# Up-projection weight factors on Trainium2: the low part made by ScalarE and an accumulating DMA in place of a VectorE subtraction

## The chip, the cores and the metric

The kernel runs on one core of one Trainium2 chip. A core has a matrix engine (TensorE, "PE" in the profile; "PEld" is its weight load), a vector engine (VectorE, "DVE"), an engine for functions of one input (ScalarE, "ACT"), GpSimd ("POOL") and SyncE ("SP"), which here only issues transfers. Transfers run on 16 DMA engines; they are issued from an engine's queue in that queue's order, and a queue whose next transfer has to wait holds back all those behind it. The metric is the time of one execution on the device in microseconds (us). Of the kernel before there are three runs: 2419.17, 2419.81 and 2420.04 us; the median is 2419.81 us.

## What is computed

A decoder layer over 2048 positions of width 1024, in float32: a first half (projections, a pooling mixer, windowed attention, gates, an output projection) and a feed-forward half. The change touches the feed-forward half's up-projection:

```python
h = rmsnorm(x, ffn_norm)                                 # (2048, 1024)
up = causal_depthwise_conv(h @ w_up, conv_w, conv_b)     # w_up: (1024, 5632), window 3
gate, val = up[..., :2816], up[..., 2816:]
x = x + (silu(gate) * val) @ w_down
```

## The kernel before

**Two parts of each number.** TensorE is fed with a reduced format (`fp32r`). A float32 number goes in as a high part (the number rounded to that format) and a low part (the number minus its high part), and a product takes three matmuls: high with high, high with low, low with high. High parts come from ScalarE as a copy that rounds (CAST); low parts come from VectorE as a subtraction of the high part from the number.

**Stages.** The 2048 positions are done in two chunks of 1024 (`c` = 0 and 1). Each chunk runs the first half of the layer, the output projection (`out_proj`), the up-projection (`up`) and the down-projection (`Down`). In the profiled execution the up-projection of chunk 0 lies at about 590 to 990 us and that of chunk 1 at about 1785 to 2195 us; the output projection of chunk 0 lies ahead of it, from about 500 us.

**One unit of the up-projection.** `up` goes over 22 units `f`. A unit takes one 128-column slab of `w_up` for the gate (`g`, 128 x 1024 numbers, 512 KB) and one for the value (`v`, likewise), and multiplies them with the normed input by a scheme of seven block products in place of eight (`one` to `seven`, 12 matmuls of 128 x 512 each). The weight side of the scheme needs factors in two parts: `A11, A12` from `g`; `A22` from the half of `v`; `S3, S2` from `v` after two in-place subtractions; and `S1, S4` from `g` after two in-place operations. Class `Blocks` makes them in four steps: `first` (A11, A12), `second` (A22, then L354 and L355 change `v` in place), `third` (S3, S2), `fourth` (L362 and L363 change `g` in place, then S1, S4). The steps `first`, `third` and `fourth` call `halved`, which takes a tile `U` of 128 x 2 x 1024, writes the high part into its first half on ScalarE (L334) and the low part into its second half on VectorE (L335). `second` splits half a slab with lines of its own (L350, L351).

**Order of the work.** In the loop over the units the four steps for unit `f+1` are called between the products of unit `f` (`weights(f + 1, 1)`), so each factor is made about a unit before the products that read it. The program is written in that order, and a scheduler places each instruction in its engine's queue; each engine then works through its queue in order, waiting on semaphores.

**Buffers and queues.** Raw slabs land in pool `rp` (tag `R`, 3 buffers); a buffer is loaded anew when its last reader has finished. All transfers of this part are issued from SP's queue by `load` (L215): the slabs (`R<-w_up`), the stored activations (`actd<-M`), and in the output projection the residual input (`F<-xT`), the weights (`R<-w_out`) and `x2d<-M`. GpSimd issues none.

**The two first units of chunk 0.** Units 0 and 1 (`PRE`) are treated apart. In chunk 0 their slabs are loaded during the output projection into one `U` tile each (`U<-w_up`), `Blocks` makes their factors there (two steps per output tile), and `store` writes the factors to device memory from SP's queue (`kept<-U`, `kept<-M`), from where both chunks fetch them (`U<-kept`). So `halved` runs 6 times in the output projection of chunk 0 and 3 times for each of 20 units in each chunk: 126 times.

Of the kernel before, what the change touches and what calls it, by code (L numbers as in the profile page):

```python
# [16 lines left out]
F32 = mybir.dt.float32  # L17
F32R = mybir.dt.float32r
I32 = mybir.dt.int32
U8 = mybir.dt.uint8  # L20
AF = mybir.ActivationFunctionType
ALU = mybir.AluOpType
# [172 lines left out]
def block_kernel(ctx: ExitStack, tc: tile.TileContext, x, xT, pos, vec, qkn, w_poolT, w_pool, w_q, w_kv,  # L195
                 w_gp, w_ga, w_out, w_up, w_down, outT):
    nc = tc.nc
    V, G, A = nc.vector, nc.gpsimd, nc.scalar
# [18 lines left out]
    def split(hi, lo, src):  # L217
# [4 lines left out]
            low = V.tensor_sub(lo[:, t], src[:, t], hi[:, t].bitcast(F32))  # L222
        return high.ins, low.ins

    def halves(h, t, src, gain):

        A.activation(h[:, 0, t], src, AF.Identity, scale=gain)
        V.scalar_tensor_tensor(h[:, 1, t], src, gain, h[:, 0, t].bitcast(F32), op0=ALU.mult,
                               op1=ALU.subtract)
# [84 lines left out]
    class Blocks:  # L314
# [16 lines left out]
        def halved(self, first, second, raw):  # L331
            t = up_.tile([P, 2, 8, P], F32R, "U")
            self.tiles.append(t)
            A.copy(t[:, 0], raw)  # L334
            V.tensor_sub(t[:, 1], raw, t[:, 0].bitcast(F32))  # L335
            self.w[first], self.w[second] = t[:, :, 0:4], t[:, :, 4:8]

        def step(self, n=1):
# [52 lines left out]
    raw = [rp.tile([P, 8, P], F32, "R") for _ in range(3)] + [mp.tile([P, 8, P], F32, "M")]  # L391
# [18 lines left out]
    def make_h(c, n, hs, ks=range(KT)):  # L410

        a, b = ((0, 256), (256, 512), (512, T))[n] if c == 0 else (0, T)
        t, w = slice(a, b), b - a
        for k in ks:
            if n == 0:
                hs.append(up_.tile([P, 2, T], F32R, "U"))
            if c == 0:
                src = xs0[k // 2][:, k % 2, t]
            else:
                src = mp.tile([P, w], F32, "M")  # L420
                load(src, xT[k * P:(k + 1) * P, c * T:(c + 1) * T])
            halves(hs[k], t, src, vc[:, V_AN + k:V_AN + k + 1])
# [1184 lines left out]
```

## Time and profile before

| What | before |
|---|---|
| median of 3 runs | 2419.81 us (2419.17 to 2420.04) |
| span of the profiled execution | 2416.4 us, first to last instruction; what lies around it to the median is 3.4 us |
| TensorE busy | 2397.1 us, 99% |
| VectorE busy | 1885.1 us, 78% |
| ScalarE busy | 1121.3 us, 46% |
| GpSimd busy | 156.2 us, 6% |
| granted TensorE clock | 0.999 of full |
| high part of `halved`, ScalarE L334 | 126 of 128 x 1024, about 1.05 us each |
| low part of `halved`, VectorE L335 | 126 of 128 x 1024, about 1.22 us each |

Reading the rows: a row of a list of windows gives the stretch and its length, then for each engine the time that it was busy and the number of its instructions, then the granted TensorE clock, the mean busy share of the 16 DMA engines and the rate that they moved. A row of the timeline gives start and duration in us, the engine, the line, the operation, output and input, and in brackets the idle time just before with what ended it. "SPq" is SP's queue issuing. TensorE's matmuls are pipelined, so the ends of its rows overlap the next starts.

### The profile page before, as it was taken

To read this page: it belongs to the slowest core of one execution; us is meant where nothing else is said; L and a number is where in the kernel's file an instruction comes from. 1 tells how busy PE (TensorE), PEld (TensorE's weight loads), DVE (VectorE), ACT (ScalarE), POOL (GpSimd) and SP (SyncE) were. 2 spreads that over 40 slices of the span, in tenths; PEclk is the share of its full clock that TensorE was granted. 3 is DMA by queue.
4 is the path that set the end of the run, shared out by engine and by line. 5 is a ranking of instruction groups with operands and counts; after the bars stand their busy time and mean duration, and the time that the engine had idled before them with its cause. 6 is when DMAs were issued, how large, how long until landed. Compare 5 with 4: busy or idle time off the path is not lost.

```text
span 2416.4 us, 30417 instructions
## 1 busy us (share of the span) xinstructions
PE 2397.1 (99%) x11252; PEld 1994.5 (83%) x11252; DVE 1885.1 (78%) x3011; ACT 1121.3 (46%) x2150; POOL 156.2 (6%) x102
## 2 busy tenths in 40 slices
PE   8999999999999999999999999999999999999999
PEld 8878888888888888788888888888888888888887
DVE  8687788765988788899956867665479878889994
ACT  7445444444554555543523433333445445554432
POOL 1113111000000000000002221110000000000000
PEclk9999999999999999999999999999999999999999
DMA  9755354268222233644334542131642222228421
GB/s 343 245 188 169 137 183 156 101 227 283 79 87 88 96 105 109 220 155 153 119 143 126 169 167 98 65 108 54 208 164 95 87 87 79 79 70 287 139 70 52
DMA packets 139028, 337.84 MB, mean 140 GB/s; under 512 B 12289, under 2 KB 48641, under 8 KB 127873
## 3 DMA queue, kind: packets, MB, share of 16 engines
q1 hardware_dynamic: 138448, 335.72, 40.8%
q8 instruction: 88, 1.44, 0.2%
q14 instruction: 60, 0.48, 0.1%
q10 hardware_dynamic: 432, 0.19, 0.0%
HBM read 231.67 MB, written 104.20 MB: 139 GB/s over the span
## 4 chain that ended last, share of the span: by engine, by line
PE 93%; DVE 3%; ACT 2%; DMA 1%; issue 1%; POOL 0%; SPq 0%; DVEq 0%; ACTq 0%; POOLq 0%
PE f L238 34%; PE f L1105 19%; PE t L1105 10%; PE a L1105 5%; PE f L1406 4%; PE a L1406 4%; PE s L1406 4%; PE t L1406 4%; PE a L887 2%; PE s L826 2%; PE a L238 1%; PE t L859 1%; DMA U<-actd 0%; DMA U<-w_down 0%; DVE F L941 0%
## 5 line engine op out<-in xcount | busy, mean ns | idle before, releaser
L238 PE MATMUL f<-U,U 128*128 128x512 f32 (+1 forms) x3936 | 916.7, 390 | 3.5 <-DVE U L222 1.9
L238 PEld LDWEIGHTS f<-U,U 128*128 128x128 f32 x3936 | 727.4, 188 | 153.6 <-DVE U L222 4.3
L1105 PE MATMUL f<-U,U 128*128 128x512 f32 x1512 | 359.8, 390 | 1.3 <-ACT Q L1123 1.3
L1105 PEld LDWEIGHTS f<-U,U 128*128 128x128 f32 x1512 | 283.4, 188 | 61.6 <-ACT Q L1123 2.2
L1171 DVE SCALAR_TENSOR_TENSOR M<-F,vc,M 128x1024 f32<-128x1024 f32 x176 | 225.2, 1282 | 126.1 <-ACT M L1168 125.7
L1105 PE MATMUL t<-U,U 128*128 128x512 f32 x1080 | 253.8, 389 | 0.9 <-ACT Q L1123 0.9
L1105 PEld LDWEIGHTS t<-U,U 128*128 128x128 f32 x1080 | 202.6, 188 | 43.4 <-ACT Q L1123 1.4
L845 ACT ACTIVATE Q<-s,st,rq 128x128 f32<-128x128 f32 x256 | 113.8, 455 | 105.9 <-DVE st L842 104.0
L334 ACT CAST U<-R 128x1024 fp32r<-128x1024 f32 x120 | 125.4, 1053 | 60.3 <-DVE R L363 29.7
L335 DVE TENSOR_TENSOR U<-R,U 128x1024 fp32r<-128x1024 f32 x120 | 146.4, 1222 | 0.0
L1105 PE MATMUL a<-U,U 128*128 128x512 f32 x576 | 139.0, 390 | 0.0
L1105 PEld LDWEIGHTS a<-U,U 128*128 128x128 f32 x576 | 108.0, 188 | 22.4
L867 POOL TENSOR_SCALAR_AFFINE_SELECT M<-M 128x1024 fp32r<-128x1024 f32 x64 | 90.6, 1416 | 542.1 <-DVE M L864 343.5
L1105 PE MATMUL f<-U,M 128*128 128x512 f32 x504 | 122.0, 390 | 0.5 <-DVE F L1149 0.5
L1364 ACT CAST U<-U 128x1024 fp32r<-128x1024 f32 x76 | 79.1, 1050 | 80.6 <-PE a L1406 25.6
L1105 PEld LDWEIGHTS f<-U,M 128*128 128x128 f32 x504 | 94.5, 188 | 20.9 <-DVE F L1149 1.3
L1168 ACT ACTIVATE M<-F,vc 128x1024 f32<-128x1024 f32 x88 | 109.4, 1243 | 1.9 <-DVE F L1153 0.5
L1157 ACT COPY F<-f 128x512 f32<-128x512 f32 x42 | 24.6, 587 | 171.0 <-PE f L1105 171.0
L222 DVE TENSOR_TENSOR U<-R,U 128x512 fp32r<-128x512 f32 x142 | 95.0, 700 | 6.9 <-ACT U L221 6.2
L1365 DVE TENSOR_TENSOR U<-U,U 128x1024 fp32r<-128x1024 f32 x76 | 92.0, 1219 | 6.3 <-ACT U L1364 6.1
L221 ACT CAST U<-R 128x512 fp32r<-128x512 f32 x142 | 80.7, 618 | 20.4 <-PE f L238 8.2
L1364 ACT CAST F<-U 128x1024 fp32r<-128x1024 f32 x44 | 46.2, 1050 | 91.4 <-PE a L1406 58.6
(273 smaller groups left out, 3620.8 us busy)
## 6 DMA issues: line engine op xcount, KB each, us to landing
R<-w_up SPq DMA_DIRECT2D x80, 512.0 KB, 3.7
actd<-M SPq DMA_DIRECT2D x44, 512.0 KB, 2.6
U<-w_down SPq DMA_DIRECT2D x88, 256.0 KB, 5.0
U<-actd SPq DMA_DIRECT2D x88, 256.0 KB, 5.4
qd<-U SPq DMA_DIRECT2D x64, 256.0 KB, 3.7
Q<-qd SPq DMA_DIRECT2D x64, 256.0 KB, 4.1
R<-w_out SPq DMA_DIRECT2D x32, 512.0 KB, 5.3
U<-kept SPq DMA_DIRECT2D x12, 1024.0 KB, 7.1
```

Of the source, the lines that this page charges most:

```text
L222: low = V.tensor_sub(lo[:, t], src[:, t], hi[:, t].bitcast(F32))
L238: nc.tensor.matmul(out, a, b, start=(i == 0), stop=(i == n - 1))
L334: A.copy(t[:, 0], raw)
L335: V.tensor_sub(t[:, 1], raw, t[:, 0].bitcast(F32))
L845: A.activation(pr[:, h, :], sc[:, h, 0:P], AF.Exp, bias=nm[:, h:h + 1], scale=it["rq"][:, h:h + 1], accum_out=rs[:, h:h + 1])
L867: G.affine_select(own.rearrange("p a h q -> p (a h) q"), pa.bitcast(F32).rearrange("p a h q -> p (a h) q"), pattern=[[0, 8], [1, P]], base ...
L1105: nc.tensor.matmul(bank, a[:, x, k, :], b[k // 2][:, y, k % 2, :], start=(first and i == 0), stop=(i == 11), skip_group_check=True)
L1168: A.activation(y, u[:, 2:], AF.Identity, bias=cw[:, 3, m:m + 1], scale=cw[:, 2, m:m + 1])
L1171: V.scalar_tensor_tensor(y, u[:, j:j + T], cw[:, j, m:m + 1], y, op0=ALU.mult, op1=ALU.add)
L1364: A.copy(hi, src)
L1365: V.tensor_sub(lo, src, hi.bitcast(F32))
L1406: nc.tensor.matmul(into[m], u[:, 0, c_], v[:, 1], start=(first and j == 0), stop=(k == n - 1 and j == 2), skip_group_check=True)
```

## The change

`halved` calls a new function `parts_added` in place of the ScalarE copy and the VectorE subtraction. ScalarE still writes the high part; then ScalarE reads the raw numbers a second time, multiplies by -1 and writes the rounded result, which is the negated high part, into the place of the low part; then GpSimd issues a DMA with `accum_op=ALU.add` that adds the raw numbers (viewed as `fp32r`) onto it. The sum is the raw number minus its high part. `second` keeps its VectorE subtraction.

```diff
+    def parts_added(hi, lo, src):
+
+        A.copy(hi, src)
+        A.activation(lo, src, AF.Copy, scale=-1.0)
+        G.dma_start(lo, src.bitcast(F32R), accum_op=ALU.add)
+
...
         def halved(self, first, second, raw):
             t = up_.tile([P, 2, 8, P], F32R, "U")
             self.tiles.append(t)
-            A.copy(t[:, 0], raw)
-            V.tensor_sub(t[:, 1], raw, t[:, 0].bitcast(F32))
+            parts_added(t[:, 0], t[:, 1], raw)
             self.w[first], self.w[second] = t[:, :, 0:4], t[:, :, 4:8]
```

In the changed file the new lines are L227 (high part), L228 (negated high part) and L229 (the DMA); lines behind them stand 6 further down, those behind `halved` 5.

**ScalarE, one unit of the steady up-projection.** Before, in ScalarE's queue (L334 are the three high parts, `third`, `fourth` and the next unit's `first`; L350 is A22's; L1123 empties PSUM banks; L1161 and L1166 carry two columns; L1168 and L1182 belong to the convolution and the gate):

```order
L350 CAST M_6967<-R_6672 128x512
L1123 COPY Q_6984<-f_6913 128x512
L1161 COPY F_7047<-uh_193 128x2
L334 CAST U_6986<-R_6672 128x1024
L1166 COPY uh_193<-F_6775 128x2
L1168 ACTIVATE M_7003<-F_6775,vc_127 128x1024
L1123 COPY Q_7030<-t_7017 128x512
L334 CAST U_7014<-R_6670 128x1024
L334 CAST U_7082<-R_6806 128x1024
L1182 ACTIVATE M_7007<-M_7003 128x1024
```

The same stretch of a unit in the changed kernel (L355, L1128, L1166, L1171, L1173 and L1187 are the lines above, shifted by 5):

```order
L355 CAST M_7276<-R_6974 128x512
L1128 COPY Q_7293<-f_7221 128x512
L1166 COPY F_7358<-uh_193 128x2
L227 CAST U_7295<-R_6974 128x1024
L228 ACTIVATE U_7295<-R_6974 128x1024
L1171 COPY uh_193<-F_7080 128x2
L1173 ACTIVATE M_7313<-F_7080,vc_127 128x1024
L227 CAST U_7324<-R_6972 128x1024
L228 ACTIVATE U_7324<-R_6972 128x1024
L1128 COPY Q_7341<-t_7328 128x512
L227 CAST U_7393<-R_7111 128x1024
L1187 ACTIVATE M_7317<-M_7313 128x1024
```

Each cast has gained a second pass behind it (that of the third cast stands behind the gate's L1187); the rest keeps its order.

**GpSimd, the steady up-projection.** Its queue was empty there; now it holds three accumulating DMAs per unit, each waiting for ScalarE and for an earlier DMA of its own kind:

```order
L229 DMA U_6420<-R_6138 128x1024 [waits DMASW5_49,DMAHW0_49,PE_49,Activation_49]
L229 DMA U_6461<-R_6140 128x1024 [waits DMASW7_49,DVE_49,DMAHW2_49,PE_49,Activation_49]
L229 DMA U_6490<-R_6138 128x1024 [waits DVE_49,DMASW6_49,PE_49,Activation_49]
L229 DMA U_6559<-R_6277 128x1024 [waits DMASW0_49,DMAHW3_49,PE_49,Activation_49]
L229 DMA U_6600<-R_6279 128x1024 [waits DMASW2_49,DVE_49,DMAHW5_49,PE_49,Activation_49]
```

"DMASW" are the semaphores of DMAs that GpSimd issued, "DMAHW" those of SP's.

**SP, the output projection of chunk 0.** The stores of unit 1's factors and what stands behind them, before:

```order
L215 DMA kept_0_47_5275<-U_5177 128x2048 [waits DMAHW2_49,Activation_49]
L215 DMA x2d_208<-M_5259 128x512 [waits DMAHW3_49,DVE_49]
L215 DMA kept_1_48_5277<-M_5180 128x1024 [waits DMAHW4_49,Activation_49]
L215 DMA kept_2_49_5279<-U_5226 128x2048 [waits DMAHW5_49,Activation_49]
L215 DMA kept_3_50_5281<-U_5231 128x2048 [waits DMAHW6_49,Activation_49]
L215 DMA x2d_208<-M_5308 128x512 [waits DMAHW7_49,DVE_49]
L215 DMA F_5321<-xT 128x512 [waits DMAHW0_49]
L215 DMA R_5323<-w_out 128x1024 [waits DMAHW1_49]
```

and in the changed kernel:

```order
L215 DMA kept_0_47_5281<-U_5180 128x2048 [waits DMAHW2_49,DMASW3_49,Activation_49]
L215 DMA x2d_208<-M_5265 128x512 [waits DMAHW3_49,DVE_49]
L215 DMA kept_1_48_5283<-M_5184 128x1024 [waits DMAHW4_49,Activation_49]
L215 DMA kept_2_49_5285<-U_5230 128x2048 [waits DMAHW5_49,DMASW4_49,Activation_49]
L215 DMA kept_3_50_5287<-U_5236 128x2048 [waits DMAHW6_49,DMASW5_49,Activation_49]
L215 DMA x2d_208<-M_5314 128x512 [waits DMAHW7_49,DVE_49]
L215 DMA F_5327<-xT 128x512 [waits DMAHW0_49]
L215 DMA R_5329<-w_out 128x1024 [waits DMAHW1_49]
```

The order here is the same; the three stores of whole `U` tiles now also wait for an accumulating DMA each, and the residual's and the weights' loads stand behind them in the queue.

## The prediction, made before the changed kernel ran

> **What bounds the kernel now.** I read the page's engine rows first, then busy time by window, then the timeline of one unit, then the queues.
>
> ```profile
> PE 2397.1 (99%) x11252; PEld 1994.5 (83%) x11252; DVE 1885.1 (78%) x3011; ACT 1121.3 (46%) x2150; POOL 156.2 (6%) x102
> ...
> L334 ACT CAST U<-R 128x1024 fp32r<-128x1024 f32 x120 | 125.4, 1053 | 60.3 <-DVE R L363 29.7
> L335 DVE TENSOR_TENSOR U<-R,U 128x1024 fp32r<-128x1024 f32 x120 | 146.4, 1222 | 0.0
> ```
>
> ```profile
> 505.00:545.00 40.00, 39.83 (x175) 32.36 (x174) 31.23 (x46) 24.84 (x40) 0.00 (x0) 1.00 0.91 330
> 545.00:590.00 45.00, 44.26 (x193) 36.21 (x192) 28.21 (x39) 20.31 (x34) 1.39 (x1) 0.96 0.83 284
> 590.00:640.00 50.00, 49.33 (x226) 40.51 (x226) 42.29 (x44) 24.19 (x36) 1.01 (x1) 1.00 0.33 119
> 640.00:990.00 350.00, 350.00 (x1544) 289.62 (x1543) 289.51 (x321) 190.21 (x296) 1.64 (x1) 1.00 0.29 95
> ...
> 1840.00:2190.00 350.00, 350.00 (x1546) 289.81 (x1545) 285.51 (x315) 178.37 (x240) 0.00 (x0) 1.00 0.28 91
> ```
>
> TensorE is busy for 2397.1 of 2416.4 us. In the two steady stretches of the up-projection (the rows of 350 us) it is busy for 350.00 of 350.00 at full clock: nothing there waits on VectorE, though VectorE is busy for 83% of it. So the work taken off VectorE is not on the path. The DMA engines are nearly idle in these stretches (0.29) and nearly full in the output projection of chunk 0 (0.91, then 0.83), where six of the 126 low parts are made. The chain of waits gives the length of a unit:
>
> ```profile
> 690.06 5.44 PE f L1105 x24
> ...
> 709.10 5.44 PE f L1105 x24
> ```
>
> Same place in two units: 19.04 us each. 24 matmuls take 5.44 us, a product of 12 takes 2.72.
>
> **What the change removes and adds.** Removed: 126 subtractions of 1.22 us, 154 us of VectorE. On the path they weigh nothing in the rows of 350 us; the largest gain left elsewhere is TensorE's idle time at the heads of the up-projection (0.67 us in 590 to 640, 0.74 in 545 to 590). I count 0, at best -1.5.
>
> Added on ScalarE: 126 second passes. The nearest row is the cast, 1.05 us, the other bound the convolution's first pass of the same size, 1.24 (below); I take 1.05, 132 us in all, three per unit. ScalarE goes from 190.21 of 350 by 18.4 units x 3.15 = 58 to 248, 71%. It stays under TensorE, and I count 0. Its order matters more: the second pass stands ahead of PSUM copies (L1123). In the unit below a bank is filled at 809.58 and used again at 815.01, 5.4 us later; two passes (2.1 us) or one with a convolution pass (2.3 us) ahead of a copy of 0.59 fit.
>
> Added on GpSimd: 126 DMAs. GpSimd was busy for 1.64 of 350 us, so their issue delays nothing of its own. What counts is L, the time from the end of the second pass to the landing, and E, the time of all 16 engines that one takes. The trace has no accumulating DMA. The nearest:
>
> ```profile
> R<-w_up SPq DMA_DIRECT2D x80, 512.0 KB, 3.7
> actd<-M SPq DMA_DIRECT2D x44, 512.0 KB, 2.6
> ...
> kept<-U SPq DMA_DIRECT2D x6, 1024.0 KB, 6.9
> ```
>
> E: a unit moves three transfers of 512 KB (two slabs, one store) and costs 0.29 x 19.04 = 5.5 us of the engines, 1.84 each. An addition reads source and destination and writes: at least 1.84, at most three such passes, 5.5; I take two, 3.7. L: at least 2.6 (the store), at most three loads, 11.1; I take 7, the row that moves twice the bytes (6.9).
>
> The Trainium skill, "Collectives: The Full Stack", The bandwidth ceiling, says that an add in the DMA engines is slow not for its arithmetic but for its two source reads on one read ring, a rate of half a copy's; by it E would be 2 x 1.84 = 3.7. No run here shows it yet.
>
> **Is it hidden in the up-projection?** One unit of the timeline:
>
> ```profile
> 806.86 2.88 PE L1105 MATMUL f<-U,U 128*128 128x512 f32 x12
> ...
> 807.67 1.24 ACT L1168 ACTIVATE M<-F,vc 128x1024 f32<-128x1024 f32 x1
> 808.82 0.60 ACT L350 CAST M<-R 128x512 fp32r<-128x512 f32 x1
> ...
> 809.58 5.60 PE L1105 MATMUL t<-U,U 128*128 128x512 f32 x24
> 809.77 0.59 ACT L1123 COPY Q<-f 128x512 f32<-128x512 f32 x1 [0.35 <-PE f L1105]
> ...
> 812.67 1.05 ACT L334 CAST U<-R 128x1024 fp32r<-128x1024 f32 x1 [0.35 <-DVE R L355]
> ...
> 815.01 5.60 PE L1105 MATMUL f<-U,U 128*128 128x512 f32 x24
> ...
> 816.91 2.08 ACT L334 CAST U<-R 128x1024 fp32r<-128x1024 f32 x2 [1.11 <-DVE R L363]
> 816.95 2.64 SPq L215 DMA_DIRECT2D R<-w_up  x2
> ```
>
> SP's own waits from 500 to 1010 us (total, times, longest) have on top:
>
> ```profile
> SPq L215 <- DVE R L363: 137.3, 18, 11.8
> ```
>
> It now waits for VectorE's last read of a slab (L363) before it loads the buffer anew. In the changed kernel the buffer is free only when the accumulating DMA that reads it has landed.
>
> - `third` (cast at 812.67): both passes end at 814.8, the low part lands at 814.8 + L. Product `three` of the next unit reads it at 806.86 + 19.04 = 825.9: it holds while L < 11.1.
> - The next `v` slab is loaded when that DMA has landed, and needs 3.7 us more; its A22 cast comes at 808.82 + 19.04 = 827.9: it holds while L < 9.4. Beyond, ScalarE waits, and behind it the copy that TensorE needs by 815.01 + 19.04 = 834.05, so TensorE feels it from about L = 14.
> - `fourth` (cast at 816.91): passes end at 819.0; product `four` reads it at 809.58 + 2.72 + 19.04 = 831.3: L < 12.3. SP's next load and the store of the activations stand behind it; their tiles are wanted half a unit later.
> - Engines: 5.5 + 3 x 3.7 = 16.6 of 19.04 us.
>
> With L = 7 all four hold, and the up-projection costs 0. The cover is thin: on the engines it is gone at E = (19.04 - 5.5) / 3 = 4.5 us.
>
> **Where it does cost: the output projection of chunk 0.** The stores of unit 1's factors wait for their low parts in SP's queue, and loads that TensorE needs at once stand behind them.
>
> ```profile
> 515.96 1.05 ACT L334 CAST U<-U 128x1024 fp32r<-128x1024 f32 x1 [2.60 <-PE f L238]
> ...
> 523.31 0.85 SPq L215 DMA_DIRECT2D U<-w_up  x2
> ...
> 529.55 1.05 ACT L334 CAST U<-U 128x1024 fp32r<-128x1024 f32 x1
> ...
> 535.89 1.99 ACT L334 CAST U<-U 128x1024 fp32r<-128x1024 f32 x2
> ...
> 541.50 1.42 SPq L215 DMA_DIRECT2D kept<-U  x2
> ...
> 544.11 0.32 SPq L215 DMA_DIRECT2D x2d<-M  x1
> 544.48 1.24 SPq L215 DMA_DIRECT2D F<-xT  x1
> ...
> 552.56 0.69 DVE L1027 SCALAR_TENSOR_TENSOR M<-f,F 128x512 f32<-128x512 f32 x1 [6.47 <-DMA F<-xT]
> ...
> 554.44 2.16 ACT L221 CAST U<-R 128x512 fp32r<-128x512 f32 x4
> ...
> 555.61 0.73 PE L238 MATMUL f<-U,U 128*128 128x512 f32 x2 [0.55 <-ACT U L221]
> ```
>
> ```profile
> 555.00:560.00 5.00, 4.26 (x13) 3.06 (x13) 3.27 (x6) 2.82 (x6) 1.39 (x1) 0.74 0.86 266
> ```
>
> The residual's load `F<-xT` is issued at 544.48 and VectorE, idle for 6.47 us, starts on it at 552.56; ScalarE's casts of the weights follow in order, and TensorE waits for them (0.55 us at 555.61): a chain without slack. After the change, `third` and `fourth` of unit 1 (casts at 535.89) end their four passes at 540.1; `fourth` lands at 547.1 with L = 7, the last store goes out then, and `F<-xT` at about 547.9 in place of 544.48: +3.4 us at TensorE. With L = 2.6 the slip is 0, with 11.1 it is 7.5.
>
> Ahead of it unit 0 does the same: its last cast (515.96) ends its second pass at 518.1 and lands at 525.1, and the loads of unit 1's slabs, behind it in the queue, slip from 523.31 to about 526.0. Unit 1's first cast stood at 529.55, one landing after those loads, so its steps slip too: 0 to +2.7, and I take half, 1.3. On top, a wait of TensorE goes with a lower clock (0.74 in the window from 555): 5 us at 0.74 lost 1.3 us for stalls of 0.73 there; longer stalls may lose as much again. I take 1.3.
>
> Sum: 0 + 0 + 0 + 3.4 + 1.3 + 1.3 = +6.0 us on the span of 2416.4, 2422.4; with the 3.4 us around it to the median, 2425.8, I say 2426 (+0.25%). Its own range, L from 2.6 to 11.1: 2418 to 2434.
>
> **Rivals.**
>
> *Hidden (not slower).* One mechanism: the addition is as quick as a copy within the chip, so the stores wait no longer than now. For it: the engines are not at their limit where they look full:
>
> ```profile
> 535.00:540.00 5.00, 5.00 (x24) 4.02 (x23) 5.00 (x7) 2.88 (x4) 0.00 (x0) 1.00 0.89 274
> 540.00:545.00 5.00, 4.83 (x21) 3.47 (x20) 3.69 (x7) 4.20 (x8) 0.00 (x0) 1.00 1.02 415
> ```
>
> With shares of 0.89 and 1.02 they move 274 and 415 GB/s; much of a share is waiting. Against it: in 505 to 545 a plain 1024 KB store takes 6.9 us. It decides where L is under 4.5 us: slip below 1 us, 2419 to 2422, I say 2420. The Trainium skill, "DMA: Bandwidth & Descriptors", Anatomy of one DMA, fits a DMA from GpSimd by 2.0 us and its bytes at 436 GB/s; an estimate by it for 512 KB is 3.2 us, which would bring this rival about. No run here shows it yet.
>
> *The additions bound the up-projection (much slower).* E at its upper bound, 5.5 us: a unit needs 5.5 + 16.6 = 22.1 us of the engines, 3.1 over 19.04, in 40 units +122 us: about 2548. Or L beyond 11.1, where `three` waits. It decides from E = 4.5 or L = 11. For it: three DMAs come within 7.4 us of each other (passes end at 814.8, 819.0 and 822), so the last waits for the others. Against it: 1.84 us per plain 512 KB already holds waiting for device memory, and the additions stay inside the chip.
>
> *Faster.* VectorE's freed time reaches TensorE: at most the 1.5 us above, 2418; over 0.2% would need 4.8 us, which the windows do not hold.
>
> **How the numbers follow.** Measured against the runs, 0.2% (4.8 us, beyond 2424.6 or below 2415.0) is what can be told from no change. My forecast, a stall of some us in the output projection: 0.40, of which 0.07 ends below 2424.6. Hidden: 0.29. Additions as the bound: 0.28, a third of it below 2500 (a thin overrun of E or L). Faster: 0.03. So slower 0.33 + 0.28 = 0.61, same 0.29 + 0.07 = 0.36, faster 0.03. The range from 2418 to 2500 leaves out two thirds of the additions as the bound and a little at its lower end, 2 in 10.
>
> **What would show it.** Right: L228 with 126 passes of about 1.05 us; the additions (`U<-R` from GpSimd) landing in 5 to 9 us; a unit still 19.04 us and 350 of 350 busy; in SP's waits `kept<-U` held by an accumulating DMA, and TensorE's idle time in 505 to 600 up from 0.9 to some 5 us. Wrong: units longer than 19.04 with TensorE waiting for a DMA or for ScalarE (the second rival), or the waits at 543 and 555 as short as before (the first).

## The result and the profile after

The changed kernel takes 2438.18 us (median of 4 runs, 2434.66 to 2440.53), the kernel before on the same chip 2419.49 us (4 runs, 2418.26 to 2420.04): 1.0079 times as long, 95% interval 1.0067 to 1.0091, or +18.7 us. It is slower, as forecast, but three times as far from the kernel before as the forecast of 2426 us, and above the forecast's own range (2418 to 2434), though inside the range of 2418 to 2500 that the second rival had opened. The profiled execution has a span of 2438.1 us, 21.7 us more than before.

The page of the changed kernel (engine rows, the DMA queue of GpSimd, groups, DMA issues):

```profile
PE 2403.7 (99%) x11252; PEld 1998.1 (82%) x11252; DVE 1755.8 (72%) x2885; ACT 1225.6 (50%) x2276; POOL 264.7 (11%) x228
...
q0 software_dynamic: 18144, 66.07, 15.2%
...
L229 POOL DMA_DIRECT2D U<-R x120 | 103.1, 859 | 749.0 <-ACT U L228 454.3
...
L228 ACT ACTIVATE U<-R 128x1024 fp32r<-128x1024 f32 x120 | 126.5, 1054 | 0.0
...
U<-R POOLq DMA_DIRECT2D x120, 512.0 KB, 5.2
R<-w_up SPq DMA_DIRECT2D x80, 512.0 KB, 5.4
actd<-M SPq DMA_DIRECT2D x44, 512.0 KB, 6.8
```

The work moved as the code says. VectorE's busy time fell by 129 us and ScalarE's rose by 104, less than the 154 and 133 that the single instructions add up to (126 of 1.222 and of 1.054 us), because the rows of neighbouring instructions overlap. An addition lands 5.2 us after its issue, and GpSimd's queue takes 15.2% of the engines' span: 0.152 x 2438.1 / 126 = 2.94 us of all 16 engines for each. (This is the time that its packets took. The engines' share reached 1.02 in a window of the prediction, so it can include waiting.) The plain transfers beside it land later than before (slab load 3.7 to 5.4, store of the activations 2.6 to 6.8).

Busy time by window, changed kernel:

```profile
505.00:545.00 40.00, 34.57 (x147) 27.47 (x146) 19.63 (x31) 23.91 (x36) 3.65 (x4) 0.97 0.96 302
545.00:590.00 45.00, 39.40 (x163) 32.12 (x162) 21.61 (x33) 19.95 (x33) 2.74 (x3) 0.88 0.85 281
...
640.00:990.00 350.00, 346.47 (x1520) 286.17 (x1520) 230.03 (x261) 233.94 (x347) 47.80 (x56) 1.00 0.74 177
...
780.00:990.00 210.00, 210.00 (x928) 173.96 (x927) 136.41 (x156) 141.57 (x213) 28.88 (x34) 1.00 0.78 186
...
1900.00:2200.00 300.00, 300.00 (x1325) 248.40 (x1324) 197.19 (x222) 190.09 (x253) 40.32 (x47) 1.00 0.69 164
```

In the steady up-projection TensorE has no idle time, at a DMA share of 0.78 in chunk 0 and 0.69 in chunk 1. The loss lies ahead of it. In 505 to 590 TensorE was idle for 85 - 84.09 = 0.91 us and is now idle for 85 - 73.97 = 11.03; and its clock there is lower (0.97 and 0.88 in place of 1.00 and 0.96), which takes another 1.0 + 4.7 - 1.8, about 4 us.

Timeline of TensorE, changed kernel: two stalls in the output projection, the first product of the up-projection, and a stall in its third unit (unit 2). Then that first product in the kernel before:

```profile
543.55 19.36 PE L244 MATMUL f<-U,U 128*128 128x512 f32 x72 [4.38 <-ACT U L221]
...
569.30 15.03 PE L244 MATMUL f<-U,U 128*128 128x512 f32 x57 [5.60 <-ACT U L221]
...
604.37 2.88 PE L1110 MATMUL f<-U,U 128*128 128x512 f32 x12
...
658.57 6.86 PE L1110 MATMUL t<-U,U 128*128 128x512 f32 x22 [3.23 <-DMA U<-R]
```

```profile
590.95 2.88 PE L1105 MATMUL f<-U,U 128*128 128x512 f32 x12
```

The up-projection of chunk 0 starts 604.37 - 590.95 = 13.4 us later. Following the starts of the later stages through both timelines, another 5.5 us come in chunk 0's up-projection (3.2 of them the wait at 658.57), none up to chunk 1's, 2.8 in chunk 1's up-projection (0.9 of them in its last unit) and none behind it: the down-projection of chunk 1 starts at 2221.10 in place of 2199.41, 21.7 us later. (The expectation of the first run below divides the last 2.8 into 1.9 and 0.9 behind the up-projection; the 0.9 still belong to it.)

The DMA queues from 505 us to that start (packets, MB, share of the 16 engines' time in the stretch), before and then changed:

```profile
q1 hardware_dynamic: 8125, 26.19, 86.7%
```

```profile
q1 hardware_dynamic: 8125, 26.19, 74.1%
q0 software_dynamic: 864, 3.15, 16.1%
```

The plain queue carries the same 8125 packets in both, and they take the same engine time: 0.867 x 85.95 = 74.5 us before, 0.741 x 99.37 = 73.6 after. The six additions come on top, 0.161 x 99.37 = 16.0 us, and the stretch is 13.4 us longer. This comparison suggested a theory that the prediction did not have: **the engines' time**. The output projection runs with its DMA engines about nine tenths busy, and what the six additions occupy lengthens it. The prediction's theory was **the held queue**: SP's queue stands still behind the stores of the factors. The held queue is there too, SP's waits from 500 to 600 us:

```profile
SPq L215 <- DMA U<-U: 22.4, 6, 5.9
```

It even lies on the chain of waits that ends in the longer stall: the last addition takes 9.17 us to land, the store and the residual's load go out behind it, and the load lands 6.83 us after its issue:

```profile
549.27 9.17 DMA U<-U
...
559.35 6.83 DMA F<-xT
...
569.30 15.03 PE f L244 x57
```

So this trace alone fits both theories, and the runs have to tell them apart.

### The profile page after: what moved, and what is told of

Read it like the earlier page. It is cut to its first block, busy times and chain, and to the rows that moved or that the text cites. A ratio compares the mean times of both kernels' runs of the same rounds, so it can differ in the third digit from the quotient of the medians.

```text
span 2438.1 us, 31038 instructions
## 1 busy us (share of the span) xinstructions
PE 2403.7 (99%) x11252; PEld 1998.1 (82%) x11252; DVE 1755.8 (72%) x2885; ACT 1225.6 (50%) x2276; POOL 264.7 (11%) x228
## 3 DMA queue, kind: packets, MB, share of 16 engines
q0 software_dynamic: 18144, 66.07, 15.2%
## 4 chain that ended last, share of the span: by engine, by line
PE 90%; DVE 4%; DMA 3%; ACT 2%; issue 1%; POOL 0%; SPq 0%; DVEq 0%; POOLq 0%; ACTq 0%
PE f L244 33%; PE f L1110 17%; PE t L1110 9%; PE a L1110 5%; PE f L1411 4%; PE a L1411 4%; PE s L1411 4%; PE t L1411 4%; PE a L892 2%; PE s L831 2%; PE a L244 1%; PE t L864 1%; DMA U<-R 1%; DMA U<-w_down 1%; DMA U<-U 0%
## 5 line engine op out<-in xcount | busy, mean ns | idle before, releaser
L229 POOL DMA_DIRECT2D U<-R x120 | 103.1, 859 | 749.0 <-ACT U L228 454.3
L227 ACT CAST U<-R 128x1024 fp32r<-128x1024 f32 x120 | 125.5, 1046 | 30.2 <-DVE R L360 29.3
L228 ACT ACTIVATE U<-R 128x1024 fp32r<-128x1024 f32 x120 | 126.5, 1054 | 0.0
L1173 ACT ACTIVATE M<-F,vc 128x1024 f32<-128x1024 f32 x88 | 109.1, 1240 | 1.9 <-DVE F L1158 0.5
L359 DVE TENSOR_TENSOR R<-R,R 128x512 f32<-128x512 f32 x40 | 27.7, 692 | 102.8 <-DMA R<-w_up 102.8
```

What stands on the lines that cost most here:

```text
L227: A.copy(hi, src)
L228: A.activation(lo, src, AF.Copy, scale=-1.0)
L229: G.dma_start(lo, src.bitcast(F32R), accum_op=ALU.add)
L1173: A.activation(y, u[:, 2:], AF.Identity, bias=cw[:, 3, m:m + 1], scale=cw[:, 2, m:m + 1])
```

## The experiments

The kernel before takes 2418.3 to 2418.8 us beside these runs. "Start" is the start of the first product of chunk 0's up-projection, 590.95 us before and 604.37 in the changed kernel.

**Where the loss sits: one place at a time.** First the changed kernel with the factors of units 0 and 1 made by VectorE again:

```diff
-            parts_added(t[:, 0], t[:, 1], raw)
+            if self.added:
+                parts_added(t[:, 0], t[:, 1], raw)
+            else:
+                A.copy(t[:, 0], raw)
+                V.tensor_sub(t[:, 1], raw, t[:, 0].bitcast(F32))
...
-                        made = Blocks([raw[:, 0], raw[:, 1]])
+                        made = Blocks([raw[:, 0], raw[:, 1]], added=False)
```

> Units 0 and 1 (made in the output projection of chunk 0) take their low parts from VectorE again; the other 120 low parts stay with the accumulating DMA. By landmarks of the two traces the start of chunk 0's up-projection came 13.5 us later, the up-projections themselves lost 5.4 and 1.9 us, the rest 0.9. If the cost ahead of the up-projection comes from the six DMAs of units 0 and 1, about 8 us stay: 2427 to 2429 against 2419.5 before. If the loss of chunk 0's up-projection only follows from its late start (transfers still crowded), less stays: 2420 to 2424.

Measured: 2427.91 us (2423.39 to 2428.56), ratio 1.0034 (1.0021 to 1.0046), start at 591.75. The output projection is as before, and half of the loss stays. (Its profiled execution was the shortest of the five, so its trace shows only some 5 of the 9.6 us.)

The opposite, only the six additions of the output projection, by the same switch:

```diff
-            return Blocks(raws)
+            return Blocks(raws, added=False)
```

> The reverse: only the six low parts of units 0 and 1 come by accumulating DMA, the other 120 from VectorE. If the two parts add up: +13.5, about 2433. If the loss ahead of the up-projection has another source than these six (the 120 later ones cannot reach back), it is near 2419.5.

Measured: 2429.37 us (2428.23 to 2430.25), ratio 1.0043 (1.0031 to 1.0056), start at 603.86. So these six cost 11.1 us and the other 120 cost 9.6; together 20.7, close to the whole of 18.7.

Then the changed kernel with units 0 to 3 made by VectorE, the additions from unit 4 on:

```diff
-            return Blocks(raws)
+            return Blocks(raws, added=key[1] > 3)
...
-                        made = Blocks([raw[:, 0], raw[:, 1]])
+                        made = Blocks([raw[:, 0], raw[:, 1]], added=False)
```

> Units 0 to 3 take their low parts from VectorE; the 38 later units of both chunks keep the accumulating DMA. Theory: what is left of the loss (8 to 10 us with units 0 and 1 back) is the ramp, where the factors of units 2 and 3 are wanted sooner after they are made than in the steady units, and the steady units hide the DMA wholly: 2418 to 2421 against 2418.3 before, and no wait of TensorE for a DMA of GpSimd. Rival: the steady units lose too, by a crowded DMA ring or by what follows: 2424 to 2428 stays.

Measured: 2420.74 us (11 runs, 2418.24 to 2422.53), ratio 1.0007 (0.9998 to 1.0016). Windows of the two up-projections:

```profile
640.00:990.00 350.00, 350.00 (x1545) 289.53 (x1544) 234.21 (x268) 234.52 (x350) 47.80 (x54) 1.00 0.73 174
1840.00:2190.00 350.00, 350.00 (x1544) 289.52 (x1543) 231.61 (x262) 221.32 (x294) 46.35 (x54) 1.00 0.70 171
```

108 of the 126 additions run beneath a TensorE that is never idle, with VectorE busy for 234 us of 350 in place of 290. Their cost is within the uncertainty (at most 3.9 us by the interval), and so is any gain from the freed VectorE. By the difference to the kernel with only units 0 and 1 made by VectorE, units 2 and 3 alone cost 2427.91 - 2420.74 = 7.2 us over both chunks, some 7 since the executions of the first lie 5 us apart: the start of the up-projection, where a factor is wanted soon after it is made.

**ScalarE's second pass.** The changed kernel, with VectorE adding in place of the DMA:

```diff
-        G.dma_start(lo, src.bitcast(F32R), accum_op=ALU.add)
+        V.tensor_add(lo, src, lo.bitcast(F32))
```

> ScalarE makes its second pass (the negated high part) 126 times as in the change, but VectorE adds the raw numbers in place of the DMA. Theory (the DMA's landing is what is waited for): 2419 to 2421, as before. Rival (ScalarE's second passes, in order ahead of what TensorE waits for): most of the loss stays, 2430 to 2438. Rival (order of the queues alone): also stays.

Measured: 2416.54 us (11 runs, 2415.49 to 2418.4), ratio 0.9992 (0.9983 to 1.0001), start at 590.86. The 126 passes cost nothing; all of the loss comes with the DMAs.

**The held queue.** The changed kernel, with the stores of the factors issued from GpSimd, so that SP's queue has no wait for an addition:

```diff
             for i, t in enumerate(self.tiles):
                 kept[f].append(dp.tile(list(t.shape), F32, f"kept_{f}_{i}"))
-                load(kept[f][-1], t.bitcast(F32))
+                G.dma_start(kept[f][-1], t.bitcast(F32))
```

> As the change, but the eight stores of units 0's and 1's factors are issued from GpSimd's queue, so that SP's queue no longer stands behind the accumulating DMAs in the output projection. Theory (SP's queue is held, loads behind it come late): the 13.5 us shrink to 0 to 4, 2425 to 2429. Rival (the additions' traffic slows the loads whichever queue waits): 2434 to 2438 stays.

Measured: 2437.41 us (2435.31 to 2439.13), ratio 1.0076 (1.0063 to 1.0089), start at 604.91: nothing is won. The loads that had been held are issued earlier (unit 1's slabs at 520.49 in place of 530.38), but land later. DMA issues of this run from 500 to 600 us, and two of TensorE's stalls:

```profile
R<-w_out SPq DMA_DIRECT2D x11, 512.0 KB, 8.2
U<-w_up SPq DMA_DIRECT2D x2, 512.0 KB, 12.4
```

```profile
537.83 0.74 PE L244 MATMUL f<-U,U 128*128 128x512 f32 x2 [3.69 <-ACT U L221]
...
554.10 0.73 PE L244 MATMUL f<-U,U 128*128 128x512 f32 x2 [3.04 <-ACT U L221]
```

The same weight loads took 6.0 us and the slabs 6.8 in this stretch of the kernel before. So the loss does not need SP's held queue. This run alone does not rule out that landings are what is waited for: GpSimd's queue is now held by the stores (unit 1's second and third additions go out at 549.77 and 552.32 in place of 545.76 and 549.27), and VectorE still waits for landings before it changes a slab in place (6.8 us in all). The next run takes these waits away.

**Additions that nobody reads.** The kernel before, with VectorE's factors, and six accumulating DMAs of the same size, each over a factor tile that has already been stored:

```diff
                 load(kept[f][-1], t.bitcast(F32))
+                if i != 1:
+                    G.dma_start(t[:, 1], t[:, 0], accum_op=ALU.add)
...
-            return Blocks(raws)
+            return Blocks(raws, added=False)
...
-                        made = Blocks([raw[:, 0], raw[:, 1]])
+                        made = Blocks([raw[:, 0], raw[:, 1]], added=False)
```

> The kernel before (all low parts from VectorE), and after each of the six stores of a whole tile of units 0 and 1 an accumulating DMA of the same size over the stored tile, which no later work reads: the same traffic as the change in the output projection, with no store and no load of the program waiting for it but the next user of the buffer. Theory (the engines' time is full there: 6 x 2.9 = 17.5 us added to a stretch with some 5 us idle): +9 to +13, 2427 to 2431. Rival (waiting for the landing, in SP's queue or at ScalarE): 2418 to 2421.

Measured: 2431.85 us (2429.55 to 2432.83), ratio 1.0051 (1.0038 to 1.0063), start at 605.33. Timeline of TensorE in this run:

```profile
535.16 8.87 PE L244 MATMUL f<-U,U 128*128 128x512 f32 x26 [3.27 <-ACT U L221]
...
569.50 15.78 PE L244 MATMUL f<-U,U 128*128 128x512 f32 x57 [7.29 <-ACT U L221]
```

By the trace no instruction waits for one of these additions, and the output projection is 14.4 us longer all the same. The chain of waits that ends in the stall of 7.29 us holds no addition; its longest piece is a load of weights (in the kernel before no load of weights from 500 to 580 us took over 8.0 us):

```profile
552.90 15.34 DMA R<-w_out
```

The loss there is what the additions do to the other transfers.

**The price of a plain copy.** The changed kernel, with the DMA copying the raw numbers in place of adding them:

```diff
-        G.dma_start(lo, src.bitcast(F32R), accum_op=ALU.add)
+        G.dma_start(lo, src.bitcast(F32R))
```

> The 126 DMAs of GpSimd copy the raw numbers in place of adding them, so the low part is the raw number and the output is not the layer's; everything else, waits too, as in the change. It measures what the addition itself costs against a copy. If an addition takes the engines twice a copy's time (2.9 against 1.5 us) and the loss ahead of the up-projection is the engines' time, six copies cost 8.8 us less 5.4 idle: 2420 to 2425. If an addition costs no more than a copy: 2435 to 2440, as the change.

Measured: 2423.76 us (10 runs, 2422.24 to 2425.15), ratio 1.0021 (1.0011 to 1.003), start at 597.91. From the page of this run:

```profile
q0 software_dynamic: 18144, 66.07, 7.7%
...
U<-R POOLq DMA_DIRECT2D x120, 512.0 KB, 3.6
```

A copy takes 0.077 x 2422.2 / 126 = 1.48 us of the engines, half of an addition's 2.94 over the same packets and bytes, and delays the start by half as much, 7.0 us. TensorE has no wait for a DMA at the start of the up-projection.

**Each addition twice.** Every low part is added to twice, the second DMA after the first:

```diff
-        G.dma_start(lo, src.bitcast(F32R), accum_op=ALU.add)
+        for _ in range(2):
+            G.dma_start(lo, src.bitcast(F32R), accum_op=ALU.add)
```

> Each of the 126 accumulating DMAs is issued twice, so the low part is twice the raw number less the high part and the output is not the layer's. Time of the 16 engines per addition, from the trace of the change: 2.9 us. Theory of the bound by engines: a unit needs 5.5 + 6 x 2.9 = 22.9 us of them in place of 19.04, +3.8 in 40 units = +154, and the output projection +30: about 2600. Rival, only the landing counts (two in a row, about 12 us, against a chain of 19.04 - 8.5 = 10.5 us for loading, changing and splitting a slab): +1.7 in 40 units = +66 and +30: about 2515. Prediction's cover wrong and both hidden: near 2450.

Measured: 2760.21 us (2757.19 to 2762.84), ratio 1.141 (1.1394 to 1.1425), start at 623.70: far above every expectation. The same product in two units in a row, and TensorE's longest waits over the run:

```profile
801.45 2.88 PE L1111 MATMUL a<-U,U 128*128 128x512 f32 x12
...
827.61 2.65 PE L1111 MATMUL a<-U,U 128*128 128x512 f32 x11
```

```profile
PE f L1111 <- DMA U<-R: 121.0, 40, 8.2
PE t L1111 <- DMA U<-R: 52.4, 29, 8.4
```

A unit takes 26.16 us in place of 19.04. The engines don't set that: they are busy for 0.76 of 640 to 990 us. The two DMAs land 6.5 us each after their issue, one behind the other, some 13 us, past the 11.1 at which product `three` begins to wait. Once it waits, the latencies form a ring (landing, next slab into the freed buffer, the operations on it, the passes, landing): in 780 to 860 us the chain of waits is 47% additions and 22% slab loads. Beside the waits, TensorE is busy for 2506.9 us in place of 2397.1, at a mean granted clock of 0.963. So in the steady units the limit is latency, it lies between one and two additions in a row, and past it the loss is large.

**Half of the six.** The kernel before, with only unit 1's three low parts made by the DMA:

```diff
-            return Blocks(raws)
+            return Blocks(raws, added=False)
...
-                        made = Blocks([raw[:, 0], raw[:, 1]])
+                        made = Blocks([raw[:, 0], raw[:, 1]], added=f == 1)
```

> The kernel before, with only the three low parts of unit 1 made by the accumulating DMA, and none elsewhere: half of the six additions of the output projection. Theory of the engines' time: 3 x 2.94 = 8.8 us of the engines against some 5 us to spare, so a loss of 3 to 6 us, 2421 to 2424 us, less than half of what all six cost (11.1). Theory that unit 1's additions alone do it because the stores of unit 1 and what stands behind them wait for their landing: the whole loss, 2428 to 2431 us. If unit 0's additions alone do it, 2418 to 2420 us.

Measured: 2424.9 us (7 runs, 2423.65 to 2427.44), ratio 1.0029 (1.0018 to 1.0039), start at 597.76. Window of this run:

```profile
505.00:590.00 85.00, 79.92 (x338) 65.09 (x337) 51.09 (x75) 44.56 (x71) 3.79 (x4) 0.94 0.86 293
```

Half of the additions delay the start by 6.8 us, half of 13.4. All three expectations missed: the loss is about proportional, with no first 5 us for free as the theory of the engines' time had it then. Put side by side (engine time is the number of DMAs times 2.94, or 1.48 for a copy):

| Run | Engine time added, us | Start later by, us | per us added |
|---|---|---|---|
| unit 1's additions alone | 8.8 | 6.8 | 0.77 |
| six copies (with all others) | 8.9 | 7.0 | 0.79 |
| six additions alone | 17.6 | 12.9 | 0.73 |
| the change | 17.6 | 13.4 | 0.76 |
| six additions, unread | 17.6 | 14.4 | 0.82 |

Each start is that of one execution, and the executions of one kernel lie 2 to 6 us apart, so the differences between the quotients mean nothing. The mean of 2.94 is also somewhat high for this stretch: here GpSimd's queue took 16.0 us in the change and 17.3 with the unread additions, which makes the quotients 0.84 and 0.83. From 505 us to the start both queues together fill 86.7% of the engines' time in the kernel before, 90.2% in the change and 90.1% with the unread additions, as if the stretch grew until the transfers fit (the run with five stores fewer, below, is the exception: 84.0%).

**Room for the additions, first try.** The changed kernel and the kernel before, each with the stores of the factors (six of 1024 KB and two smaller) issued in the second half of the output projection's tiles:

```diff
-                    elif m == at + 3:
-                        made.store(f)
+                    if m == at + 3:
+                        late[f] = made
+                if c == 0 and n == 1 and m in (1, 2):
+                    late[m - 1].store(m - 1)
```

> The changed kernel, but the three stores of the factors of unit 0 and the three of unit 1 are no longer issued inside the output projection of chunk 0 as soon as the factors are made, but at its last weight tile, after the loads that TensorE needs. Six stores of 1024 KB leave the crowded stretch from 505 to 575 us and nothing else changes. Theory of the engines' time: the six additions cost 6 x 2.94 = 17.6 us of the 16 engines and the stretch had some 5 us to spare; six stores of 1024 KB free more than that, so the output projection loses 0 to 5 us in place of 13.5, and with the 8 us of the rest of the loss the kernel takes 2424 to 2431 us. Theory that it is a wait of TensorE's work for one landing, whatever else the engines carry: little changes, 2434 to 2440.

> The kernel before with the same later stores, as the control for the run beside it. TensorE was idle for 0.9 us between 505 and 590 us in the kernel before and lost about a microsecond to the lower clock there, so at most 2 us are to be had: 2416 to 2419 us by either theory. If it takes much less, the stores and not the additions had been the load to look at; if it takes more, the later stores cost something where they now stand, and the run beside it has to be read with that.

Measured: with the change 2435.34 us (2433.38 to 2436.76), ratio 1.0071 (1.0057 to 1.0084), start at 601.00. Without it 2413.58 us (11 runs, 2412.5 to 2414.49), ratio 0.9981 (0.9972 to 0.999), start at 587.80. SP's timeline with the change shows why the first tells nothing between the theories: the first and the last of the six large stores are issued at

```profile
517.08 0.33 SPq L215 DMA_DIRECT2D kept<-U  x1
...
570.58 0.38 SPq L215 DMA_DIRECT2D kept<-U  x1
```

They moved back, but not out of the crowded stretch. The later stores are worth 3 us of start in either kernel, and the change costs 13.2 us of start with them as without. The window of the kernel before with later stores:

```profile
505.00:590.00 85.00, 85.00 (x382) 70.52 (x381) 60.23 (x85) 46.30 (x76) 1.01 (x1) 1.00 0.89 317
```

Its TensorE is busy for all of 85 us at full clock. This version, without the change, is faster than both kernels by the measure of these runs.

**Room for the additions, second try.** The changed kernel, with five of the six stores left out:

```diff
             for i, t in enumerate(self.tiles):
+                if i != 1 and "one" in kept:
+                    kept[f].append(kept["one"])
+                    continue
...
+                if i == 0:
+                    kept["one"] = kept[f][-1]
```

> The changed kernel with five of the six 1024 KB stores of the factors of units 0 and 1 left out; where those factors are loaded back at the start of the up-projection, the one tile that is still stored is read in place of all six. So the values of the up-projection's first two units are not the reference's, and everything else is as in the changed kernel, the loads back with their sizes too. Unlike the run with the later stores, which left all six stores between 517 and 571 us, this one takes 5 x 2 x 1.84 = 18.4 us of the engines' time out of the output projection, about what the six additions bring in, 6 x 2.94 = 17.6 us. Theory of the engines' time: the output projection loses 0 to 3 us in place of 13.5, the up-projection starts at 588 to 594 us, and the kernel takes 2422 to 2429 us with the ramp's loss still in it. Theory that each addition costs its two microseconds as a wait for its own landing, whatever else the engines carry: the start stays at 600 to 605 us and the kernel at 2433 to 2440 us.

Measured: 2429.76 us (2428.47 to 2431.88), ratio 1.0047 (1.0034 to 1.0061). The queues from 505 us to the start, and TensorE's two longest stalls and that start:

```profile
q1 hardware_dynamic: 7396, 20.88, 65.7%
q0 software_dynamic: 864, 3.15, 18.3%
```

```profile
536.11 12.83 PE L244 MATMUL f<-U,U 128*128 128x512 f32 x48 [2.42 <-ACT U L221]
551.15 0.73 PE L244 MATMUL f<-U,U 128*128 128x512 f32 x2 [2.22 <-ACT U L221]
...
596.68 2.88 PE L1115 MATMUL f<-U,U 128*128 128x512 f32 x12
```

The start falls between the two expectations. The plain queue takes 0.657 x 91.68 = 60.2 us in place of 73.6, so the stores freed 13.4 and not the 18.4 that I had put down; that gave 7.7 of the 13.4 us back. Both queues together now take 77.0 us, 2.5 more than the kernel before, yet the start is 5.7 us later than there. At 0.76 the 2.5 us are worth 2. So the engines' time explains most of the loss, but not the remaining 3 to 4 us. These may belong to where the additions stand: in this run too TensorE stalls at 522 and 536 us, behind three additions issued from 510 to 520 us, where only two of the five stores are missing. That is argued, not shown.

## Why the prediction was right in sign and short in size

- **VectorE's 154 us (129 of busy time) are worth nothing: right.** TensorE is at 350.00 of 350 with VectorE at 290 (before) and at 234 (additions from unit 4 on).
- **ScalarE's second pass is worth nothing: right.** 1.054 us each against 1.05 forecast; with VectorE adding after it, the ratio is 0.9992.
- **E, 3.7 us: sized too high, reasoned right.** 2.94 measured. The step "two passes of a plain transfer" holds: an addition takes 2.94 / 1.48 = 2.0 times a copy within the chip. The pass was too large: 1.84 came from transfers to and from device memory. The rule quoted from the Trainium skill ("Collectives: The Full Stack", The bandwidth ceiling), half of a copy's rate because of two source reads, is told there of the add in a reduce-scatter and agrees with this ratio; that the read ring is the reason no run here shows.
- **L, 7 us: too long in one place, too short in the other.** 5.2 at the median, 8.8 in the output projection. The fit quoted from the Trainium skill ("DMA: Bandwidth & Descriptors", Anatomy of one DMA) had given 3.2: near the copy's 3.6, not the addition's 5.2.
- **"The up-projection costs 0": right for its steady units, wrong for its first.** The conditions (L below 11.1, 9.4, 12.3) were worked out at one steady unit and held there. The step never looked at the first units that are made inside the up-projection. There `fourth` of unit 2 is issued at 649.37 us and lands 9.15 us later, and TensorE waits till 658.57. By the runs, units 2 and 3 cost 7.2 us.
- **The output projection, +6.0: the failed step.** It was sized by how far SP's queue is held. The hold came, at the places that were named, and longer than forecast (526.0 and 547.9); the changed kernel's timeline of SP has unit 1's slabs at 530.38 in place of 523.31 and the residual's load at 559.35 in place of 544.48:

```profile
530.38 2.14 SPq L215 DMA_DIRECT2D U<-w_up  x2
...
559.35 0.90 SPq L215 DMA_DIRECT2D F<-xT  x1
```

  But with the hold taken away nothing was won, and with additions that nobody waits for all of the loss came. The up-projection starts 13.4 us later where the sum had 6.0. The engines' time was in the prediction, as E, and was summed for the up-projection only, where the share was 0.29. Summed for the output projection it would have been 6 x 3.7 = 22 us brought into 85 us that were at 0.91 and 0.83: the sentence "much of a share is waiting" set that aside. It may be waiting, but it is not free: 0.73 to 0.82 us were lost for each us brought in. A rest stays open: the run with five stores fewer got back only 7.7 of the 13.4 us.
- **The lower clock, +1.3: too small.** About 4 us, as the stalls were longer.
- **The rivals.** Hidden falls: L was above 4.5. The additions as the bound of the up-projection falls: E is under 4.5 and L under 11.1. The doubled additions show that of its two conditions L was the one to watch: by the engines a unit would have taken 5.5 + 6 x 2.85 = 22.6 us (2.85 us for an addition in that run), and it took 26.16.
- **The range.** The wide one held by luck, because of a rival whose mechanism did not come; the forecast's own, 2418 to 2434, did not, since it varied L alone.

## What to carry to other kernels

Before work is moved to the DMA engines, add up what it occupies of them stage by stage, and hold it against the busy share of each stage: in this stage, at nine tenths, some three quarters to four fifths of it came out at the end, even where nothing waited for the moved work. A median over steady units says nothing on the first units of a stage, where the same landing has no unit's worth of cover. An engine that is not on the path is no reason to move its work: 129 us less of VectorE were worth nothing here.

## What the runs showed of the hardware

- An accumulating DMA of 512 KB within the chip takes twice the engines' time of a copy (2.94 and 1.48 us) over the same packets and bytes, and lands in 5.2 us where a copy takes 3.6.
- Beside SP's transfers, the additions in GpSimd's queue had 39 to 52% of the engines' time (39.4% from 515 to 525 us, 51.5% from 550 to 560) and moved about half as much with it. The shares of the second stretch add up to 103%, so packets' times overlap a little. The queues of the changed kernel from 550 to 560 us:

```profile
q1 hardware_dynamic: 471, 2.07, 51.6%
q0 software_dynamic: 282, 1.02, 51.5%
```

- Plain transfers land later beside additions even where the engines have time to spare: the store of the activations 6.8 us in place of 2.6, where the mean share is 0.74 (640 to 990 us).
- When TensorE restarted at 569.30 us, after a stall of 5.60 us, its granted clock was at half, and back at full some 4.5 us later. Windows of the changed kernel:

```profile
568.00:570.00 2.00, 0.70 (x2) 0.50 (x2) 1.24 (x3) 2.00 (x5) 0.13 (x1) 0.50 0.96 221
570.00:572.00 2.00, 2.00 (x6) 1.53 (x5) 1.25 (x3) 0.29 (x1) 0.00 (x0) 0.50 0.85 279
572.00:574.00 2.00, 2.00 (x8) 1.59 (x7) 0.69 (x1) 1.11 (x2) 0.00 (x0) 0.70 0.75 293
574.00:576.00 2.00, 2.00 (x11) 1.65 (x9) 1.83 (x3) 1.21 (x3) 0.00 (x0) 1.00 0.94 240
```
